# A decoder trunk on one core: the feed-forward norms by one matmul of ones and a power on 512 columns

## The chip, the cores and the metric

The kernel runs on 1 core of one Trainium2 chip. Its time is the device time of one execution in microseconds. TensorE (PE) does the matmuls, with its weight loads shown apart (PEld); VectorE (DVE), ScalarE (ACT) and GpSimd (POOL) do the rest of the arithmetic; SyncE (SP) and GpSimd issue most of the transfers. The median of three runs before is 1825.48 us (1823.81 to 1827.0).

## The reference

Two layers of a decoder trunk, 512 positions of 1024 numbers in float32, and a last norm. Each layer is a half-step feed-forward, a mixer and another half-step feed-forward, each behind an RMS norm:

```python
def _rmsnorm(x, g):
    y = xf * lax.rsqrt(jnp.mean(xf * xf, axis=-1, keepdims=True) + EPS)
    return (y * g.astype(jnp.float32)).astype(x.dtype)

def _swiglu(x, w_gate, w_up, w_down):
    return (jax.nn.silu(x @ w_gate) * (x @ w_up)) @ w_down

def _layer(x, ...):
    x = x + MACARON * _swiglu(_rmsnorm(x, ffn1_norm), ffn1_w_gate, ffn1_w_up, ffn1_w_down)
    h = _rmsnorm(x, mix_norm)
    p = h @ w_in
    ...                                     # three mixers on parts of p
    x = x + jnp.concatenate([y_a, y_b, y_c], axis=-1) @ w_out
    x = x + MACARON * _swiglu(_rmsnorm(x, ffn2_norm), ffn2_w_gate, ffn2_w_up, ffn2_w_down)
    return x
```

The feed-forwards are 1024 to 2816 and back. So there are six norms in the layers (four of feed-forwards, two of mixers) and the final one.

## The kernel before, in words

x lies on the chip transposed: features on the 128 partitions, the 512 positions along the columns, eight tiles of 128 features in four pairs. Every float32 operand of a large matmul is split into a high part (a cast on ScalarE) and a low part (a subtraction on VectorE, L90), and a product is three matmuls: high by high, high by low, low by high (L150 to L152, L257 to L259).

A feed-forward (`ffn`, and `last_ffn` in the last layer) works through the gate's and the up projection's columns in 22 "quads" q: 11 blocks of columns, gate (j = 0) and up (j = 1) in turn. A quad is seven products of half size (n = 1 to 7, Strassen's scheme with Winograd's sums), twelve matmuls of 128x256 each. `begin(q)` takes the quad's weights from a raw buffer, makes sums of them and splits them (`forms`), and fetches those of the next quad (`fetch`): four transfers a quad, three issued by SyncE and one, which adds to what is already there, by GpSimd (L112). There are two raw buffers.

The norm is put off behind the projections. x times the gain goes into the matmuls, and the result is multiplied by the reciprocal root of the mean square afterwards. That is `done(q)`: of a gate quad the whole tile is multiplied by the rows `rr` (L338), goes through Silu on ScalarE (L339), and is multiplied by `rr` again (L340); of an up quad the tile is multiplied by the gate (L343), and split into what the down projection takes.

`squares(m)` sums the squares of x over the eight tiles into `acc`, 128x512; the sum over the partitions is still to be done. The norm does it in two steps. `norm_columns` makes 128 positions at a time a column: four matmuls of acc by a column of ones give 128x4 in PSUM, VectorE divides by 1024 and adds epsilon (`ms`), and GpSimd raises it to the power -1/2 (`rc`, L230). `norm_rows` makes rows of the columns: four diagonal matrices (`dg`, L240) and four matmuls of ones by them (`psr`, L241) give every partition the same row of 512 numbers, which ScalarE copies (`rr`, L243). The mixers use both `rc` and `rr`.

In three feed-forwards the two steps are taken out of the list `norms` behind the first two products that follow the opening ones of quads 0 and 1. In the very first (`from_start`), the first two quads are computed by plain products in `start`, with the squares behind them; there the list has places to wait, and its last entry calls `norm_rows` and then `done(0)` and `done(1)`.

The order of instructions on each engine is not the order of the code: a scheduler sets it when the program is built. Each engine then works its own queue in order and waits at an instruction until what that needs is there.

Of the kernel before, what the change touches and what calls it, by code (L numbers as in the profile page):

```python
# [9 lines left out]
F32 = mybir.dt.float32  # L10
F32R = mybir.dt.float32r
AF = mybir.ActivationFunctionType
ALU = mybir.AluOpType
AX = mybir.AxisListType

P = 128
D = 1024
T = 512
# [8 lines left out]
EPS = 1e-6  # L27
# [21 lines left out]
def trunk(ctx, tc, xt, w_gu1, w_dn1, w_in, w_out, w_gu2, w_dn2, w_last, par, con, wst, bst, gain, out):  # L49
    nc = tc.nc  # L50
# [3 lines left out]
    spool = ctx.enter_context(tc.tile_pool(name="spool", bufs=2))  # L54
# [3 lines left out]
    def bank(name):  # L58
        return pp.tile([P, T], F32, tag="ps", name=name)
# [6 lines left out]
    def uniq(s):  # L66
        uid[0] += 1
        return f"{s}{uid[0]}"
# [8 lines left out]
    ones = cpool.tile([P, P], F32, name="ones")  # L77
    nc.vector.memset(ones, 1.0)
    mhalf = cpool.tile([P, 16], F32, name="mhalf")
# [77 lines left out]
    state = {}  # L157
# [12 lines left out]
    def scratch(i, name):  # L170

        if stage["tags"] is None:
            return big(uniq(name))
        if i == 2:
            return stage["pool"].tile([P, 4 * T], F32, tag="hp", name=uniq(name), bufs=4)
        return stage["pool"].tile([P, 2 * T], F32, tag=stage["tags"][i], name=uniq(name), bufs=2)
# [56 lines left out]
    def norm_rows():  # L233

        rc = state["rc"]
        pr = bank(uniq("psr"))
        dg = scratch(2, "dg")
        for n in range(NCH):
            d = dg[:, n * P : (n + 1) * P]
            nc.vector.tensor_scalar(d, ident, rc[:, n : n + 1], None, ALU.mult)  # L240
            nc.tensor.matmul(pr[:, n * P : (n + 1) * P], lhsT=ones, rhs=d, start=True, stop=True)  # L241
        rr = spool.tile([P, T], F32, tag="rr", name=uniq("rr"), bufs=1)
        nc.scalar.copy(rr, pr)  # L243
        state["rr"] = rr

    MOVING = {1: A11, 2: A12, 3: Z4, 4: A22, 5: S1, 6: S2, 7: S3}
# [26 lines left out]
    def gate_up(w_gu, first, others, tail, from_start=False):  # L275

        quads = [(p, j) for p in range(FP) for j in range(2)]
        steps = [(7 * q + t, 0, q, n) for q in range(len(quads)) for n, t in WHEN.items()]
        steps += [(t, 1, None, work) for t, work in others]
        steps.sort(key=lambda e: e[:2])
        live, gates, raws = {}, {}, {}

        def ahead(q):
            if q < len(quads) and q not in raws:  # L290
                raws[q] = fetch(w_gu[quads[q][0], quads[q][1]])

        def begin(q):
            p, j = quads[q]
            ahead(q)
            c = stage["pool"].tile([P, 2 * T], F32, tag="gu"[j], name=uniq("gu"[j]), bufs=2)
            live[q] = {"w": forms(raws[q]), "c": c}
            ahead(q + 1)

        def quarter(q, i):  # L300
            return live[q]["c"][:, i * H : (i + 1) * H]

        def psum(q, name):
            if name not in live[q]:
                live[q][name] = bank(uniq(name))[:, :H]
            return live[q][name]

        def matmuls(q, n, pairs=range(KP)):
            name = {1: "pa", 2: "pb", 3: "pc", 4: "pa", 5: "pc", 6: "pa", 7: "pa"}[n]
            fresh_bank = name not in live[q]  # L310
            product(psum(q, name), n, live[q]["w"], fresh_bank, pairs)

        def after(q, n):
            c11, c21, c12, c22 = [quarter(q, i) for i in range(4)]
            b = live[q]
            if n == 1:
                nc.scalar.copy(c11, b["pa"])  # L317
            elif n == 2:
                nc.vector.tensor_tensor(c11, b["pb"], c11, ALU.add)
            elif n == 6:  # L320
                nc.scalar.copy(c12, b["pa"])
            elif n == 5:
                nc.scalar.copy(c22, b["pc"])
            elif n == 7:
                nc.vector.tensor_tensor(c22, c22, b["pa"], ALU.subtract)
            elif n == 3:
                nc.vector.tensor_tensor(c12, b["pc"], c12, ALU.subtract)
            else:
                nc.scalar.copy(c21, b["pa"])
                done(q)  # L330

        def done(q):
            p, j = quads[q]
            c = live.pop(q)["c"]
            if j == 0:
                c3 = c.rearrange("p (f t) -> p f t", f=2)
                rr = state["rr"].unsqueeze(1).broadcast_to([P, 2, T])
                nc.vector.tensor_tensor(c3, c3, rr, ALU.mult)  # L338
                nc.scalar.activation(c, c, AF.Silu)  # L339
                nc.vector.tensor_tensor(c3, c3, rr, ALU.mult)  # L340
                gates[p] = c
            else:
                nc.vector.tensor_tensor(c, c, gates.pop(p), ALU.mult)  # L343
                h = stage["pool"].tile([P, 4 * T], F32R, tag="hp", name=uniq("h"), bufs=4)
                parts(h[:, : 2 * T], h[:, 2 * T :], c)
                for i in range(2):
                    first.append((h[:, i * T : (i + 1) * T], h[:, (2 + i) * T : (3 + i) * T]))

        if from_start:
            norms = start(w_gu, live, done)  # L350
            skip = lambda q, n: q < 2
        else:
            begin(0)
            begin(1)
            for m in range(KP):
                for q in (0, 1):
                    for n in (1, 2):
                        ps = psum(q, ("pa", "pb")[n - 1])
                        hi, lo = live[q]["w"][n]
                        bh, bl = form(m, MOVING[n])  # L360
                        c = slice(m * P, (m + 1) * P)
                        mm3(ps, hi[:, c], lo[:, c], bh, bl, m == 0, m == KP - 1, skip_group_check=True)
            for q in (0, 1):
                for n in (1, 2):
                    after(q, n)
            norms = [norm_columns, norm_rows]
            skip = lambda q, n: q < 2 and n < 3
        for _, kind, q, n in steps:
            if kind:
                n()  # L370
                continue
            if skip(q, n):
                continue
            if q not in live:
                begin(q)
            matmuls(q, n)
            if norms:
                norms.pop(0)()
            after(q, n)
        tail()  # L380

    def start(w_gu, live, done):

        for k in range(12):
            warm = warm_ps[:, (k % 4) * P : (k % 4 + 1) * P]
            nc.tensor.matmul(warm, lhsT=ones, rhs=ones, start=True, stop=True)
        pool = stage["pool"]  # L390
        extra = pool.tile([P, 4 * T], F32R, tag="hp", name="a21", bufs=4)
        a21 = [(extra[:, m * H : (m + 1) * H], extra[:, (4 + m) * H : (5 + m) * H]) for m in range(KP)]
        weights = {}
        for m in range(KP):
            nc.sync.dma_start(xp[m], xt[:, 2 * m : 2 * m + 2, :])
            norm_pair(m, G1, True)
            gained(m, 0, G1, a21[m][0], a21[m][1], slice(H, T))
            if m == 0:
                weights[0] = load_plain(w_gu[0, 0])
        weights[1] = load_plain(w_gu[0, 1])  # L400
        for m in range(KP):
            norm_sums(m, G1)
        for j in range(2):
            b11, b21, b22, b12 = weights[j]
            ps = [bank(uniq("pg")) for _ in range(2)]
            for m in range(KP):
                c = slice(m * P, (m + 1) * P)
                kw = {"skip_group_check": True}
                for i, w in ((0, b21), (1, b22)):
                    hi, lo = xf[m][:, H : 3 * H], xf[m][:, 8 * H : 10 * H]  # L410
                    mm3(ps[i], w[0][:, c], w[1][:, c], hi, lo, m == 0, False, **kw)
                for i, w in ((0, b11), (1, b12)):
                    for t, a in ((slice(0, H), form(m, A11)), (slice(H, T), a21[m])):
                        mm3(ps[i][:, t], w[0][:, c], w[1][:, c], a[0], a[1], False, m == KP - 1, **kw)
            c = pool.tile([P, 2 * T], F32, tag="gu"[j], name=uniq("gu"[j]), bufs=2)
            for i in range(2):
                nc.scalar.copy(c[:, i * T : (i + 1) * T], ps[i])
            live[j] = {"c": c}
        for m in range(KP):
            squares(m)  # L420

        def rows():
            norm_rows()
            done(0)
            done(1)

        wait = lambda: None
        return [wait] * 5 + [norm_columns] + [wait] * 2 + [rows]

    def schedule(l, w_dn, hs):  # L430

# [433 lines left out]
```

## Time and profile before

| | |
|---|---|
| median of three runs | 1825.48 us |
| the profiled execution | 1829.11 us |
| its span, first to last instruction | 1827.3 us |
| TensorE busy | 1808.7 us |
| VectorE busy | 1328.3 us |
| ScalarE busy | 832.2 us |
| GpSimd busy | 121.0 us |
| granted clock of TensorE, mean | 0.994 |

Times of the trace count from the span's first instruction. A row of a timeline gives start, duration, engine, line, operation, what is written and read, and in brackets how long the engine had been idle before and what it waited for. The four feed-forward norms stand at about 47, 575, 925 and 1478 us.

### The profile page before, as it was taken

To read this page: it belongs to the slowest core of one execution; us is meant where nothing else is said; L and a number is where in the kernel's file an instruction comes from. 1 tells how busy PE (TensorE), PEld (TensorE's weight loads), DVE (VectorE), ACT (ScalarE), POOL (GpSimd) and SP (SyncE) were. 2 spreads that over 40 slices of the span, in tenths; PEclk is the share of its full clock that TensorE was granted. 3 is DMA by queue.
4 is the path that set the end of the run, shared out by engine and by line. 5 is a ranking of instruction groups with operands and counts; after the bars stand their busy time and mean duration, and the time that the engine had idled before them with its cause. 6 is when DMAs were issued, how large, how long until landed. Compare 5 with 4: busy or idle time off the path is not lost.

```text
span 1827.3 us, 28699 instructions
## 1 busy us (share of the span) xinstructions
PE 1808.7 (99%) x11704; PEld 1655.4 (91%) x11704; DVE 1328.3 (73%) x1818; ACT 832.2 (46%) x1222; POOL 121.0 (7%) x120
## 2 busy tenths in 40 slices
PE   9999999999999999999999999999999999999998
PEld 8999999888889999999899999998888899999997
DVE  7877777675667777777878777766757678777765
ACT  6544444413345544444655444444133555444444
POOL 0100000000100000000000000000000000000000
PEclk9999999999999999999999999999999999999999
DMA  7655555522223765555446655564222157655532
GB/s 214 183 162 150 148 148 153 180 81 82 73 89 81 185 167 156 156 156 155 128 106 178 162 155 156 156 175 128 92 81 81 58 128 190 168 156 156 154 89 81
DMA packets 120339, 251.20 MB, mean 137 GB/s; under 512 B 9744, under 2 KB 11792, under 8 KB 119696
## 3 DMA queue, kind: packets, MB, share of 16 engines
q1 hardware_dynamic: 96672, 204.25, 34.6%
q0 software_dynamic: 23392, 45.09, 14.9%
q8 instruction: 91, 1.49, 0.3%
q14 instruction: 40, 0.33, 0.1%
q10 hardware_dynamic: 144, 0.04, 0.0%
HBM read 247.24 MB, written 2.10 MB: 136 GB/s over the span
## 4 chain that ended last, share of the span: by engine, by line
PE 93%; DVE 3%; DMA 2%; ACT 1%; issue 1%; SPq 0%; POOL 0%; POOLq 0%; ACTq 0%
PE pa L257 8%; PE pa L259 8%; PE pa L258 8%; PE pdn L150 8%; PE pdn L151 8%; PE pdn L152 8%; PE pc L259 4%; PE pc L257 4%; PE pc L258 4%; PE pb L257 2%; PE pb L259 2%; PE pb L258 2%; PE pqk L150 2%; PE pqk L152 2%; PE pout L150 2%; PE pout L152 2%
## 5 line engine op out<-in xcount | busy, mean ns | idle before, releaser
L150 PE MATMUL pdn<-h,wdn 128*128 128x512 f32 x632 | 248.2, 393 | 0.0
L151 PE MATMUL pdn<-h,wdn 128*128 128x512 f32 x632 | 248.0, 392 | 0.0
L152 PE MATMUL pdn<-h,wdn 128*128 128x512 f32 x632 | 246.6, 390 | 0.3 <-DVE wdn L90 0.3
L89 ACT CAST wd<-rawq 128x1024 fp32r<-128x1024 f32 (+1 forms) x172 | 135.0, 832 | 176.6 <-PE pc L259 171.3
L257 PE MATMUL pa<-xf,wa 128*128 128x256 f32 x688 | 196.5, 286 | 3.7 <-ACT u L317 2.9
L89 ACT CAST wdn<-rawd 128x512 fp32r<-128x512 f32 (+1 forms) x152 | 97.0, 638 | 218.0 <-PE pdn L152 189.0
L259 PE MATMUL pa<-xf,wa 128*128 128x256 f32 x688 | 195.8, 285 | 0.0
L258 PE MATMUL pa<-xf,wa 128*128 128x256 f32 x688 | 195.7, 284 | 0.0
L90 DVE TENSOR_TENSOR wd<-rawq,wd 128x1024 fp32r<-128x1024 f32 (+1 forms) x172 | 157.4, 955 | 49.3 <-ACT wd L89 49.1
L112 POOL DMA_DIRECT2D rawq<-in_w_gu x86 | 94.3, 1096 | 1271.3 <-DMA rawq<-in_w_gu 580.1
L89 ACT CAST w<-raw 128x1024 fp32r<-128x1024 f32 x77 | 80.9, 1051 | 196.3 <-PE pqk L152 60.6
L152 PEld LDWEIGHTS pdn<-h,wdn 128*128 128x128 f32 x632 | 119.0, 188 | 26.9 <-DVE wdn L90 1.1
L90 DVE TENSOR_TENSOR w<-raw,w 128x1024 fp32r<-128x1024 f32 x77 | 94.1, 1223 | 64.6 <-ACT w L89 63.9
L150 PEld LDWEIGHTS pdn<-h,wdn 128*128 128x128 f32 x632 | 119.6, 189 | 21.2
L151 PEld LDWEIGHTS pdn<-h,wdn 128*128 128x128 f32 x632 | 119.6, 189 | 19.6
L257 PEld LDWEIGHTS pa<-xf,wa 128*128 128x128 f32 x688 | 133.2, 194 | 4.5 <-ACT u L317 3.3
L258 PEld LDWEIGHTS pa<-xf,wa 128*128 128x128 f32 x688 | 133.3, 194 | 0.0
L259 PEld LDWEIGHTS pa<-xf,wa 128*128 128x128 f32 x688 | 133.1, 194 | 0.0
L90 DVE TENSOR_TENSOR wdn<-rawd,wdn 128x512 fp32r<-128x512 f32 (+1 forms) x152 | 107.0, 705 | 23.9 <-ACT wdn L89 23.9
L273 DVE SCALAR_TENSOR_TENSOR x<-pdn,x 128x512 f32<-128x512 f32 x152 | 104.1, 685 | 3.7 <-PE pdn L152 3.6
L90 DVE TENSOR_TENSOR wb<-rawq,wb 128x1024 fp32r<-128x1024 f32 x86 | 104.9, 1220 | 2.4 <-ACT wb L89 2.4
L90 DVE TENSOR_TENSOR wa<-rawq,wa 128x1024 fp32r<-128x1024 f32 x86 | 104.9, 1220 | 1.8 <-ACT wa L89 1.8
(289 smaller groups left out, 5080.9 us busy)
## 6 DMA issues: line engine op xcount, KB each, us to landing
rawq<-in_w_gu SPq DMA_DIRECT2D x172, 512.0 KB, 5.4
rawq<-in_w_gu POOLq DMA_DIRECT2D x86, 512.0 KB, 5.8
rawd<-in_w_dn SPq DMA_DIRECT2D x140, 256.0 KB, 5.0
raw<-in_w_in SPq DMA_DIRECT2D x52, 512.0 KB, 3.5
rawq<-in_w_gu SPq DMA_DIRECT2D x86, 256.0 KB, 5.9
raw<-in_w_out SPq DMA_DIRECT2D x16, 512.0 KB, 3.5
rawd<-in_w_dn SPq DMA_DIRECT2D x12, 384.0 KB, 3.3
raw<-in_w_last SPq DMA_DIRECT2D x6, 512.0 KB, 4.4
```

Source lines behind the costliest of these rows:

```text
L89: nc.scalar.copy(hi, src)
L90: nc.vector.tensor_tensor(lo, src, hi.bitcast(F32), ALU.subtract)
L112: nc.gpsimd.dma_start(two[:, :, 1, :], src.rearrange("p (n s c) -> p n s c", n=2, s=2)[:, :, 0, :], accum_op=ALU.add)
L150: nc.tensor.matmul(ps, lhsT=ah, rhs=bh, start=first, stop=False, **kw)
L151: nc.tensor.matmul(ps, lhsT=ah, rhs=bl, start=False, stop=False, **kw)
L152: nc.tensor.matmul(ps, lhsT=al, rhs=bh, start=False, stop=last, **kw)
L257: nc.tensor.matmul(ps, lhsT=hi[:, c], rhs=bh, start=one, stop=False, skip_group_check=True)
L258: nc.tensor.matmul(ps, lhsT=hi[:, c], rhs=bl, start=False, stop=False, skip_group_check=True)
L259: nc.tensor.matmul(ps, lhsT=lo[:, c], rhs=bh, start=False, stop=m == pairs[-1], skip_group_check=True)
L273: nc.vector.scalar_tensor_tensor(x[d], p, 0.5, x[d], ALU.mult, ALU.add)
```

## The change

The four feed-forward norms are computed by a new function, `norm_rows_alone`; the mixers keep `norm_columns` and `norm_rows`. One matmul with a 128x128 matrix of ones as the stationary operand sums `acc` over the partitions, and gives every partition the same row of 512 sums. VectorE divides by 1024 and adds epsilon, out of PSUM into `rr`; GpSimd raises `rr` in place to the power -1/2, 128x512 numbers. The tile of the diagonals is not needed there.

```diff
+    def norm_rows_alone():
+
+        ps = bank(uniq("psr"))
+        nc.tensor.matmul(ps, lhsT=ones, rhs=state["acc"], start=True, stop=True)
+        rr = spool.tile([P, T], F32, tag="rr", name=uniq("rr"), bufs=1)
+        nc.vector.tensor_scalar(rr, ps, 1.0 / D, EPS, ALU.mult, ALU.add)
+        nc.gpsimd.tensor_tensor(rr, rr, mhalf[:, 0:1].broadcast_to([P, T]), ALU.pow)
         state["rr"] = rr
...
-            norms = [norm_columns, norm_rows]
+            norms = [norm_rows_alone]
             skip = lambda q, n: q < 2 and n < 3
...
         def rows():
-            norm_rows()
+            norm_rows_alone()
             done(0)
             done(1)

         wait = lambda: None
-        return [wait] * 5 + [norm_columns] + [wait] * 2 + [rows]
+        return [wait] * 6 + [rows]
```

The lines behind the new function move down by nine: L338 becomes L347, L340 L349, L319 L328, L325 L334, L327 L336. Two places of the new order matter to what follows.

VectorE's queue in the second feed-forward, before, from the scaling of the norm's columns to the first reader of `rr`. `g` and `u` are the result tiles of the first gate and up quad, `wb` holds two operands of the second quad's weights, `wd` three of the third quad's; "waits" names the engine or transfer whose signal an instruction waits for:

```order
L228 TENSOR_SCALAR ms_5206<-pss_5201 128x4 [waits PE_49]
L240 TENSOR_SCALAR dg_5225<-ident,rc_5208 128x128 [waits Pool_49]
L319 TENSOR_TENSOR g_5095<-pb_5137,g_5095 128x256 [waits Activation_49]
L319 TENSOR_TENSOR u_5114<-pb_5145,u_5114 128x256 [waits Activation_49]
L240 TENSOR_SCALAR dg_5225<-ident,rc_5208 128x128 x3
L325 TENSOR_TENSOR g_5095<-g_5095,pa_5133 128x256 [waits PE_49,Activation_49]
L90 TENSOR_TENSOR wb_5125<-rawq_5109,wb_5125 128x1024 [waits Activation_49]
L327 TENSOR_TENSOR g_5095<-pc_5211,g_5095 128x256 [waits PE_49]
L90 TENSOR_TENSOR wd_5320<-rawq_5128,wd_5320 128x1024 [waits DMAHW3_49,Activation_49]
L90 TENSOR_TENSOR wd_5320<-rawq_5128,wd_5320 128x512 [waits DMAHW4_49,Activation_49]
L127 TENSOR_TENSOR rawq_5128<-rawq_5128 128x512 [waits DMASW6_49,DVE_49]
L130 TENSOR_TENSOR rawq_5128<-rawq_5128 128x512 [waits DVE_49]
```

The same stretch now, up to the first reader of `rr`:

```order
L251 TENSOR_SCALAR rr_5187<-psr_5185 128x512 [waits PE_49]
L328 TENSOR_TENSOR g_5079<-pb_5121,g_5079 128x256 [waits Activation_49]
L328 TENSOR_TENSOR u_5098<-pb_5129,u_5098 128x256 [waits Activation_49]
L334 TENSOR_TENSOR g_5079<-g_5079,pa_5117 128x256 [waits PE_49,Activation_49]
L90 TENSOR_TENSOR wb_5109<-rawq_5093,wb_5109 128x1024 [waits Activation_49]
L336 TENSOR_TENSOR g_5079<-pc_5191,g_5079 128x256 [waits PE_49]
L90 TENSOR_TENSOR wd_5288<-rawq_5112,wd_5288 128x1024 [waits DMAHW3_49,Activation_49]
L90 TENSOR_TENSOR wd_5288<-rawq_5112,wd_5288 128x512 [waits DMAHW4_49,Activation_49]
L127 TENSOR_TENSOR rawq_5112<-rawq_5112 128x512 [waits DMASW6_49,DVE_49]
L130 TENSOR_TENSOR rawq_5112<-rawq_5112 128x512 [waits DVE_49]
L347 TENSOR_TENSOR g_5079<-g_5079,rr_5187 128x1024 [waits Activation_49,Pool_49]
L334 TENSOR_TENSOR u_5098<-u_5098,pa_5125 128x256 [waits PE_49]
```

The diagonals are gone, and with them the wait for GpSimd at VectorE's second instruction; the wait for GpSimd now stands at L347, behind the same low parts and sums as before. The third and fourth feed-forwards have the same order here.

GpSimd's queue in the same place, before:

```order
L112 DMA rawq_5128<-in_w_gu 128x2x512 [waits DMAHW2_49,DMAHW6_49,DMASW4_49,DVE_49]
L230 TENSOR_TENSOR rc_5208<-ms_5206,mhalf 128x4 [waits DVE_49]
L112 DMA rawq_5333<-in_w_gu 128x2x512 [waits DMAHW3_49,DMAHW5_49,DMASW5_49,DVE_49]
L112 DMA rawq_5450<-in_w_gu 128x2x512 [waits DMAHW0_49,DMAHW3_49,DMASW6_49,DVE_49]
L112 DMA rawq_5566<-in_w_gu 128x2x512 [waits DMAHW3_49,DMAHW6_49,DMASW7_49,DVE_49]
```

And now:

```order
L112 DMA rawq_5112<-in_w_gu 128x2x512 [waits DMAHW2_49,DMAHW6_49,DMASW4_49,DVE_49]
L252 TENSOR_TENSOR rr_5187<-rr_5187,mhalf 128x512 [waits DVE_49]
L112 DMA rawq_5301<-in_w_gu 128x2x512 [waits DMAHW3_49,DMAHW5_49,DMASW5_49,DVE_49]
L112 DMA rawq_5418<-in_w_gu 128x2x512 [waits DMAHW0_49,DMAHW3_49,DMASW6_49,DVE_49]
L112 DMA rawq_5534<-in_w_gu 128x2x512 [waits DMAHW3_49,DMAHW6_49,DMASW7_49,DVE_49]
```

The power keeps its place between the third quad's fetch and the fourth's; only its size changes.

## Rows read from the trace of the kernel before

**Rows 1.** The page, busy time by engine: us (share of the span) xinstructions

```profile
PE 1808.7 (99%) x11704; PEld 1655.4 (91%) x11704; DVE 1328.3 (73%) x1818; ACT 832.2 (46%) x1222; POOL 121.0 (7%) x120
```

**Rows 2.** Powers by line: ns min/median/max, first and last start, shapes

```profile
L532 POOL TENSOR_TENSOR rf<-r,mhalf x4: 539/548/574, 1810.0 to 1822.3; 128x1 f32<-128x1 f32 x4
L769 POOL TENSOR_TENSOR rs<-var,mhalf x10: 1006/1008/2899, 455.4 to 1392.2; 128x4 f32<-128x4 f32 x8, 128x16 f32<-128x16 f32 x2
```

**Rows 3.** VectorE's timeline behind powers of 4, 16 and 1 columns

```profile
370.56 0.87 DVE L240 TENSOR_SCALAR dg<-ident,rc 128x128 f32<-128x128 f32 x4 [1.16 <-POOL rc L230]
...
458.29 1.23 DVE L770 TENSOR_TENSOR side<-side,rs 128x1024 f32<-128x1024 f32 x1 [3.01 <-POOL rs L769]
...
1814.73 0.49 DVE L534 TENSOR_SCALAR o<-o,rf 128x512 f32<-128x512 f32 x1 [0.67 <-POOL rf L532]
```

**Rows 4.** Timeline, VectorE and GpSimd: the two powers that took longer

```profile
48.55 1.23 DVE L90 TENSOR_TENSOR wd<-rawq,wd 128x1024 fp32r<-128x1024 f32 x1
48.73 1.96 POOL L230 TENSOR_TENSOR rc<-ms,mhalf 128x4 f32<-128x4 f32 x1 [8.39 <-DVE ms L228]
...
479.14 0.69 DVE L685 TENSOR_TENSOR sg<-yn,sg 128x512 f32<-128x512 f32 x1
479.31 1.39 POOL L769 TENSOR_TENSOR rs<-var,mhalf 128x4 f32<-128x4 f32 x1 [0.95 <-DVE mean L761]
```

**Rows 5.** Timeline, TensorE in the second feed-forward

```profile
574.95 1.05 PE L226 MATMUL pss<-ones,acc 128*128 128x1 f32 x8 [0.39 <-DVE acc L219]
...
578.82 1.05 PE L241 MATMUL psr<-dg,ones 128*128 128x128 f32 x8
...
584.26 0.28 PE L259 MATMUL pc<-xf,wb 128*128 128x256 f32 x1
...
592.90 0.28 PE L259 MATMUL pa<-xf,wa 128*128 128x256 f32 x1
```

**Rows 6.** Timeline, VectorE and GpSimd in the second feed-forward

```profile
576.04 0.16 DVE L228 TENSOR_SCALAR ms<-pss 128x4 f32<-128x4 f32 x1
576.30 1.03 POOL L230 TENSOR_TENSOR rc<-ms,mhalf 128x4 f32<-128x4 f32 x1 [3.06 <-DVE ms L228]
...
582.42 1.23 DVE L90 TENSOR_TENSOR wb<-rawq,wb 128x1024 fp32r<-128x1024 f32 x1 [0.59 <-ACT wb L89]
583.56 0.42 DVE L327 TENSOR_TENSOR g<-pc,g 128x256 f32<-128x256 f32 x1
...
587.50 1.22 DVE L338 TENSOR_TENSOR g<-g,rr 128x1024 f32<-128x1024 f32 x1 [0.34 <-ACT g L329]
...
588.98 1.22 DVE L90 TENSOR_TENSOR wa<-rawq,wa 128x1024 fp32r<-128x1024 f32 x1
```

**Rows 7.** Timeline, GpSimd and TensorE in the third and fourth feed-forwards

```profile
926.16 1.04 POOL L230 TENSOR_TENSOR rc<-ms,mhalf 128x4 f32<-128x4 f32 x1 [26.89 <-DVE ms L228]
...
935.62 0.28 PE L259 MATMUL pc<-xf,wb 128*128 128x256 f32 x1
...
1479.48 1.03 POOL L230 TENSOR_TENSOR rc<-ms,mhalf 128x4 f32<-128x4 f32 x1 [2.99 <-DVE ms L228]
...
1487.44 0.28 PE L259 MATMUL pc<-xf,wb 128*128 128x256 f32 x1
```

**Rows 8.** Timeline, TensorE in the first feed-forward

```profile
66.17 0.28 PE L257 MATMUL pa<-xf,wa 128*128 128x256 f32 x1
```

**Rows 9.** Windows: stretch, length, busy of PE, PEld, DVE, ACT, POOL, granted clock, transfers

```profile
6.00:8.00 2.00, 0.00 (x0) 0.00 (x0) 1.84 (x5) 1.80 (x4) 0.00 (x0) 1.00 0.99 408
8.80:15.20 6.40, 6.21 (x20) 5.20 (x21) 6.40 (x12) 6.40 (x14) 0.00 (x0) 0.50 0.96 352
49.20:52.80 3.60, 3.60 (x20) 3.60 (x19) 2.62 (x8) 0.00 (x0) 2.11 (x2) 0.53 0.82 262
```

**Rows 10.** The page: GpSimd's fetches (busy, mean ns); their size, median us to landing

```profile
L112 POOL DMA_DIRECT2D rawq<-in_w_gu x86 | 94.3, 1096 | 1271.3 <-DMA rawq<-in_w_gu 580.1
...
rawq<-in_w_gu POOLq DMA_DIRECT2D x86, 512.0 KB, 5.8
```

More of the change, by code (lines that the diff above doesn't have):

```diff
@@ L244, in norm_rows @@
         state["rr"] = rr
+    def norm_rows_alone():
[4 more added lines that the diff above has]
+        nc.gpsimd.tensor_tensor(rr, rr, mhalf[:, 0:1].broadcast_to([P, T]), ALU.pow)
+        state["rr"] = rr
     MOVING = {1: A11, 2: A12, 3: Z4, 4: A22, 5: S1, 6: S2, 7: S3}
```

## The prediction, made before the changed kernel ran

> **What bounds the kernel now.** I read the page's engine totals first: TensorE is busy for 1808.7 of the 1827.3 us span, VectorE for 73%, GpSimd for 7% [rows 1]. Whatever makes TensorE wait is therefore paid in full, and nothing later gives it back. Next I asked the trace for GpSimd's instructions by shape, since the change gives that engine 128 times as many columns [rows 2], and then for the instructions that waited for them [rows 3]. Last I read the timelines of TensorE, VectorE and GpSimd around the norms that change, for two things: how long after the norm TensorE runs on work that doesn't need it, and which VectorE instruction meets it first [rows 5 to 8].
>
> **What is removed and added.** Only the four feed-forward norms change; the two of the mixers keep their columns and diagonal. Each loses two groups of eight TensorE passes, busy for 1.05 us each [rows 5], a 0.16 us scaling and four diagonal products on VectorE, a 4-column power, and a copy on ScalarE. It gains one float32 matmul of 512 columns, a scaling of 512 columns and a power of 512 columns. The matmul is work of the kind and amount of the second removed group (four times 128 columns), so TensorE saves about the first group, 0.9 us; as TensorE then stands still, this saving is swallowed. The scaling is costed by VectorE's 0.49 us for 128x512 [last of rows 3] in place of 0.16 us, so +0.34 us on the path.
>
> **The power, the term that decides.** GpSimd needed 548 ns for 1 column, 1008 for 4 and 2899 for 16 (the medians, and the longest) [rows 2]. From 1 to 4 that is 153 ns a column, from 4 to 16 it is 158, from 1 to 16 it is (2899 - 548)/15 = 156.7. So 512 columns take 2.90 + 496 x 0.1567 = 80.6 us; the two other slopes give 78.8 and 81.1. These are not just a profiler's rough ends: VectorE's waits behind them grow alike, 0.67, 1.16 and 3.01 us [rows 3], or 156 ns a column from first to last. From below, no row forbids that a long operand runs no longer than the 16 columns did, 2.9 us. I take 80.6, since three points lie on one line.
>
> The Trainium skill ("GPSIMD Engine Reference", 3.1 Elementwise) gives some 2.6 cycles an element at 1.2 GHz for a two-input operation; an estimate from that page is 1.1 us for 512 columns, and by it the change would cost nothing (third rival). The rows of this power, 156 ns a column, are some 70 times dearer, and I go by the rows.
>
> **What stands behind it.** In the second feed-forward the new power can begin at 576.30 + 0.34 = 576.64 and ends at 657.24. VectorE's first reader of the norm's rows is the scaling of the first gate (L338 before, L347 now), which before started at 587.50 [rows 6]. Behind it on VectorE stand the subtraction for the other quad, the low parts of the next quad's weights and all that follows; on ScalarE the Silu, with the copies and casts behind it; on GpSimd the next weight fetch; on SyncE the fetch after that, when a buffer comes free. TensorE uses the first low part behind the reader at 592.90 [rows 5].
>
> But VectorE may stop sooner. The trace shows that a power and a VectorE instruction with two operands in SBUF don't run side by side: the power at 48.73 found such a low part (48.55, 1.23 us) running and took 1.96 us, that is 1.01 us after its end; the one at 479.31 found one of 0.69 us and took 1.39 [rows 4]. No row shows the other order, VectorE waiting for a running power, since a power of 1 us has no such instruction behind it. I take it to be the same both ways. Then in the last three feed-forwards VectorE stands not at L347 but at the low part of the second quad's weights, which started at 582.42 [rows 6] and which TensorE reads at 584.26 [rows 5]. The Trainium skill ("SBUF — State Buffer", Who interferes with whom) says just that: GpSimd and a VectorE instruction with two SBUF inputs share a port, and the first to come holds it for its whole instruction. The rows above agree for one direction; no run here shows the other.
>
> **The sum.** Second feed-forward: the power ends at 657.24, the low part takes 1.2 us, TensorE goes on at 658.44 where before it was at 584.26: +74.2 us. Third: 926.16 + 0.34 + 80.6 + 1.2 = 1008.3 against 935.62: +72.7. Fourth: 1479.48 + 82.14 = 1561.62 against 1487.44: +74.2 [rows 7].
>
> First feed-forward: its two first quads are finished from the start, so the order is another. Before, its power was begun at 48.73 [rows 4]; the wider scaling and a low part that now stands ahead of it make that about 49.3. The power ends at 129.9. Then VectorE does seven instructions of 1024 columns (1.2 us each), three of 512 (0.7) and one of 256 (0.4), 10.9 us [rows 4, 6], before the next quad's low part is there, at 140.8. Twenty matmuls later (0.12 us each: 72 of them lie between 584.26 and 592.90) TensorE is where it was at 66.17 [rows 8], and four matmuls further: 143.2 - 66.65 = +76.6.
>
> Clock: after TensorE had stood still from 6 to 8 us it was granted 0.50 from 8.80 to 15.20, the lower level of 1.2 GHz; a stretch right behind the first norm lasted 3.6 us at 0.53 [rows 9]. At half rate that loses 1.7 to 3.2 us a restart. I take 2.4, four times, 9.6 us.
>
> Hidden behind the restart: VectorE then needs 7.7 us to the next quad's low part (1.2 + 0.4 + 1.9 + 1.4 + 1.2 + 0.4 + 1.2), and TensorE reaches it 1.2 + 72 x 0.12 = 9.8 us after the power. The fetch behind the power takes 1.1 us on GpSimd and lands 5.8 us after that [rows 10], so 6.9 us after the power, and VectorE gets to its data some 12.8 us after (five more instructions, 5.1 us). Neither adds anything; a microsecond beyond these covers would be paid.
>
> Total: 76.6 + 74.2 + 72.7 + 74.2 + 9.6 = 307.3 us on a profiled execution of 1829.1 us, so 2136. That execution lay 3.6 us above the median of the runs, 1825.5; against the median it is **2133 us**.
>
> **Rivals.**
> *VectorE goes on beside the power (28%).* Then only L347 and what is behind it waits. For: no row shows the port held against VectorE. Against: the two powers that did wait. Second feed-forward: 657.24 plus the 1.5 us from that reader's start to the low part's start (587.50 to 588.98 before) plus 1.2 us = 659.9, against 592.90 [rows 5, 6]: +67.0. The other two lose as much less as this one, 7.2 us; the first about as before. Sum 307 - 22 = 285, time 2110 us.
>
> *The stall costs more than once (6%).* The weight fetch on GpSimd's queue stands behind the power, and were its data to come last after the restart, TensorE would stop again. It decides from 5.9 us (12.8 - 6.9) of delay on; at 6 us beyond that, four times, 2133 + 24 = 2157 us. Against: the queue is empty then and the median landing is 5.8 us.
>
> *The power of many columns streams (6%), the other side.* With 2.9 to 4 us it ends by about 581, 6 us ahead of L338's 587.50; nothing waits, TensorE is rid of 0.9 us in each feed-forward, and of about 1.7 us in the stretch at 0.53 if the column matmuls had a part in it. 1825.5 - 3.6 = 1822 us, or 1820. The point from which it turns is a power of about 6 us: where the port is held the low part at 582.42 comes late from there, otherwise from about 11. Against it stand three points on one line.
>
> *Something between (4%)*: a cost per column that falls with length, say 40 us a power, 1825.5 + 4 x 34 = 1960 us.
>
> **How the numbers follow.** Forecast 56%, the rest as given. Port held and not held lie close together, 2133 and 2110; with the slopes' ends (4 x 1.8 us down, 4 x 0.6 up) and the clock's (4 x 0.8) they span about 2098 to 2145. I let the range go from 2098 to 2152; what it leaves out are the streaming and the falling power and most of the repeated stall. About 0.2%, 4 us, is what a measurement of this kernel tells from no change. The streaming power gives half faster, half the same, 3% each; all else is slower, 94%.
>
> **What the new profile would show.** Four powers on GpSimd of 79 to 82 us, each behind a matmul of the sum; TensorE idle for some 70 us behind each, released through VectorE; VectorE waiting for GpSimd at its first two-input instruction in three of them (or at L347 in all, if the port is free); a granted clock of 0.5 for a few us after each restart; GpSimd busy 320 us more than now. A power of a few microseconds would make the forecast wrong from the root; powers of 80 us with TensorE hardly idle would mean that I misread what stands behind VectorE's wait.

## The result and the profile after

The changed kernel takes 2112.39 us (median; 2111.43 to 2113.99), the kernel before on the same chip 1826.24 us: a ratio of 1.1573, 95% interval 1.1550 to 1.1596. The profiled execution took 2111.58 us, its span is 2109.7 us, the mean granted clock 0.928.

The page first: busy time by engine, and the shares of the chain that ended last.

```profile
PE 1807.7 (86%) x11648; PEld 1652.3 (78%) x11648; DVE 1326.6 (63%) x1802; ACT 829.9 (39%) x1218; POOL 443.6 (21%) x120
...
PE 80%; POOL 16%; DVE 2%; issue 1%; ACT 1%; DMA 0%; POOLq 0%; SPq 0%; ACTq 0%
```

Against [rows 1], TensorE has as much work as before and is idle for 302 us of the span instead of 19. GpSimd has 323 us more, and holds 16% of the chain. The next rows are the page's groups: the new power, the first reader of its rows, and the Silu.

```profile
L252 POOL TENSOR_TENSOR rr<-rr,mhalf 128x512 f32<-128x512 f32 x4 | 327.8, 81960 | 43.5 <-DVE rr L251 43.5
...
L347 DVE TENSOR_TENSOR g<-g,rr 128x1024 f32<-128x1024 f32 x44 | 53.9, 1225 | 366.1 <-POOL rr L252 298.4 <-ACT g L338 67.7
...
L348 ACT ACTIVATE g<-g 128x1024 f32<-128x1024 f32 x44 | 46.4, 1056 | 292.7 <-DVE g L347 292.7
```

One power takes 81.96 us where one of 16 columns took 2.9 [rows 2], and VectorE waits 298.4 us for the four; the Silu on ScalarE waits 292.7 us for VectorE's L347 behind it. The waits of TensorE (total, times, longest) say how that reaches it:

```profile
PE pa L266 <- ACT g L326: 209.4, 4, 69.7
PE pc L266 <- ACT wb L89: 78.2, 1, 78.2
```

That is 78.2 us in the first feed-forward and about 69.6 us in each of the others. The engines' timelines in the second, where [rows 5, 6] show it before:

```profile
651.74 1.12 PE L249 MATMUL psr<-acc,ones 128*128 128x512 f32 x2 [0.40 <-DVE acc L219]
...
652.90 0.69 DVE L251 TENSOR_SCALAR rr<-psr 128x512 f32<-128x512 f32 x1
...
653.68 81.96 POOL L252 TENSOR_TENSOR rr<-rr,mhalf 128x512 f32<-128x512 f32 x1 [3.37 <-DVE rr L251]
...
735.67 1.23 DVE L347 TENSOR_TENSOR g<-g,rr 128x1024 f32<-128x1024 f32 x1 [72.64 <-POOL rr L252]
...
737.15 1.22 DVE L90 TENSOR_TENSOR wa<-rawq,wa 128x1024 fp32r<-128x1024 f32 x1
...
736.93 1.06 ACT L348 ACTIVATE g<-g 128x1024 f32<-128x1024 f32 x1 [70.18 <-DVE g L347]
737.90 0.35 ACT L326 COPY g<-pa 128x256 f32<-128x256 f32 x1
...
738.30 0.58 PE L266 MATMUL pa<-xf,wa 128*128 128x256 f32 x1 [69.62 <-ACT g L326]
```

The power ends at 735.64 and VectorE starts L347 at once. Nothing that TensorE waits for needs the norm. It waits for ScalarE's copy L326, which frees a PSUM bank, and that copy stands in ScalarE's queue behind the Silu, which needs L347. Read upward, the chain is power, L347, Silu, copy, matmul. TensorE stopped at 738.30 - 69.62 = 668.68, 15.0 us after the power began, and goes on 2.7 us behind its end.

In the first feed-forward TensorE waits for a cast of weights (`wb`, L89), which stands in the same queue behind the Silu:

```profile
131.39 1.06 ACT L348 ACTIVATE g<-g 128x1024 f32<-128x1024 f32 x1 [79.71 <-DVE g L347]
...
133.56 1.04 ACT L89 CAST wb<-rawq 128x1024 fp32r<-128x1024 f32 x1
...
134.65 0.58 PE L266 MATMUL pc<-xf,wb 128*128 128x256 f32 x1 [78.20 <-ACT wb L89]
```

Windows of the first stall, of the time from each restart until the clock is back, and of a stretch behind that (length, busy of PE, PEld, DVE, ACT, POOL, granted clock, DMA share, GB/s):

```profile
60.00:130.00 70.00, 0.00 (x0) 0.00 (x0) 0.00 (x0) 0.00 (x0) 70.00 (x1) 0.50 0.00 0
...
134.65:142.04 7.39, 5.92 (x24) 5.34 (x25) 7.39 (x10) 4.22 (x6) 0.00 (x0) 0.50 0.03 6
738.30:742.78 4.48, 4.48 (x21) 4.48 (x22) 4.48 (x7) 1.79 (x3) 0.00 (x0) 0.50 0.93 192
1155.41:1159.21 3.80, 3.80 (x18) 3.80 (x19) 3.80 (x6) 1.79 (x3) 0.00 (x0) 0.50 1.01 210
1776.40:1780.43 4.03, 4.03 (x19) 4.03 (x20) 4.03 (x6) 1.80 (x3) 0.00 (x0) 0.50 0.98 199
...
743.00:745.00 2.00, 2.00 (x19) 2.00 (x18) 1.42 (x3) 0.51 (x2) 0.29 (x1) 1.00 0.95 340
```

From 60 to 130 only GpSimd works. Behind each stall TensorE runs for 3.8 to 5.9 us at 0.50, the level of 1.2 GHz. Half of that time is lost, 9.1 us in the four.

### The profile page after: what moved, and what is told of

It reads as the page before. It is cut to its first block, busy times and chain, and to the rows that moved or that the text cites. A ratio compares the mean times of both kernels' runs of the same rounds, so it can differ in the third digit from the quotient of the medians.

```text
span 2109.7 us, 28571 instructions
## 1 busy us (share of the span) xinstructions
PE 1807.7 (86%) x11648; PEld 1652.3 (78%) x11648; DVE 1326.6 (63%) x1802; ACT 829.9 (39%) x1218; POOL 443.6 (21%) x120
## 4 chain that ended last, share of the span: by engine, by line
PE 80%; POOL 16%; DVE 2%; issue 1%; ACT 1%; DMA 0%; POOLq 0%; SPq 0%; ACTq 0%
POOL rr L252 16%; PE pa L266 7%; PE pa L267 7%; PE pa L268 7%; PE pdn L150 7%; PE pdn L151 7%; PE pdn L152 7%; PE pc L268 4%; PE pc L267 4%; PE pc L266 4%; PE pb L267 2%; PE pb L266 2%; PE pb L268 2%; PE pqk L150 1%; PE pqk L151 1%; PE pout L151 1%
## 5 line engine op out<-in xcount | busy, mean ns | idle before, releaser
L252 POOL TENSOR_TENSOR rr<-rr,mhalf 128x512 f32<-128x512 f32 x4 | 327.8, 81960 | 43.5 <-DVE rr L251 43.5
L347 DVE TENSOR_TENSOR g<-g,rr 128x1024 f32<-128x1024 f32 x44 | 53.9, 1225 | 366.1 <-POOL rr L252 298.4
L89 ACT CAST wd<-rawq 128x1024 fp32r<-128x1024 f32 (+1 forms) x172 | 135.3, 832 | 174.7 <-PE pc L268 170.6
L89 ACT CAST wdn<-rawd 128x512 fp32r<-128x512 f32 (+1 forms) x152 | 96.9, 638 | 212.5 <-PE pdn L152 191.6
L266 PE MATMUL pc<-xf,wb 128*128 128x256 f32 x344 | 99.4, 289 | 78.2 <-ACT wb L89 78.2
L348 ACT ACTIVATE g<-g 128x1024 f32<-128x1024 f32 x44 | 46.4, 1056 | 292.7 <-DVE g L347 292.7
L89 ACT CAST w<-raw 128x1024 fp32r<-128x1024 f32 x77 | 80.9, 1051 | 196.1 <-PE pqk L152 60.6
```

Source lines behind the costliest of these rows:

```text
L89: nc.scalar.copy(hi, src)
L252: nc.gpsimd.tensor_tensor(rr, rr, mhalf[:, 0:1].broadcast_to([P, T]), ALU.pow)
L266: nc.tensor.matmul(ps, lhsT=hi[:, c], rhs=bh, start=one, stop=False, skip_group_check=True)
```

## The experiments

My theory was by then: all of the loss is the power's length, 0.159 us a column, and it is paid beyond a fixed cover, since L347 waits in VectorE's queue and the Silu in ScalarE's. The rivals: that the new order or the wide matmul has a part in it, that the price goes by numbers and not by columns, and my own forecast, that VectorE is also shut out by the port. The variants without the power, with the square root and with the logarithm have the median of twelve executions; the others ran once.

**Without the power.**

```diff
-        nc.vector.tensor_scalar(rr, ps, 1.0 / D, EPS, ALU.mult, ALU.add)
-        nc.gpsimd.tensor_tensor(rr, rr, mhalf[:, 0:1].broadcast_to([P, T]), ALU.pow)
+        nc.vector.tensor_scalar(rr, ps, 1e-3 / D, EPS, ALU.mult, ALU.add)
```

> The changed kernel without the four powers; the scaling divides by 1024000 instead of 1024, so the rows of the norm are not the norm here: the reciprocal root is what is left out. Theory A (all of the loss is the wait for the power, the rest of the change is a small gain): TensorE has no idle stretch of more than about 3 us at the norms, and the time is that of the kernel before less four times the 0.9 to 1.2 us of TensorE's work that the one matmul saves, 1821 to 1823 us. Theory B (part of the loss is the new order of the queues or the matmul of 512 columns itself): the time stays above that of the kernel before, 1830 us or more.

Measured: 1820.01 us beside 1826.60 for the kernel before, ratio 0.9969 (0.9956 to 0.9982). Theory A holds, and the rest of the change is a gain of 6.6 us, more than the 3.6 to 4.8 that I gave it: the time lies just under the range. The profile shows TensorE busy for

```profile
PE 1800.2 (99%) x11648; PEld 1644.9 (91%) x11648; DVE 1326.2 (73%) x1802; ACT 829.5 (46%) x1218; POOL 115.7 (6%) x116
```

of a span of 1815.9. That closes the sum for the power: the changed kernel's span is 293.8 us longer, 286.3 of it more idle time (302.0 against 15.7) and 7.5 more busy time. The four restarts lose 9.1 us by the clock; against that, this run had the lower clock for longer in its opening (0.51 from 7.67 to 14.50, the changed kernel 0.52 from 8.80 to 12.30).

Part of the 6.6 us may be the clock too. The kernel before was granted half the clock in three more stretches of some 3.5 us: at 49.2 [rows 9], at 626 and at 926. This kernel had none of them, and the changed one has none but behind its stalls. I thought the column matmuls the likely cause; the rows don't bear that out. The first two lines are of the kernel before, the third of this one, the last of the variant with the square root below:

```profile
575.00:579.00 4.00, 4.00 (x34) 4.00 (x35) 2.74 (x8) 0.57 (x2) 1.03 (x1) 1.00 0.52 93
626.00:629.50 3.50, 3.50 (x14) 2.92 (x13) 3.50 (x7) 1.35 (x3) 0.00 (x0) 0.52 0.62 159
...
17.00:1810.00 1793.00, 1787.58 (x11591) 1633.63 (x11589) 1313.21 (x1777) 814.78 (x1196) 114.50 (x109) 1.00 0.51 137
...
59.50:66.00 6.50, 4.65 (x22) 4.44 (x23) 6.50 (x9) 2.52 (x5) 0.00 (x0) 0.61 0.25 63
```

The second norm's column matmuls ran at 1.00. The stretch at 626 has no norm near it, and follows a wait of TensorE of 1.99 us. The variant with the root has no such matmuls there and was granted 0.61 for 6.5 us. What brings these stretches stays open.

**Powers of 64, 128, 256 and 384 columns.**

```diff
-        nc.vector.tensor_scalar(rr, ps, 1.0 / D, EPS, ALU.mult, ALU.add)
-        nc.gpsimd.tensor_tensor(rr, rr, mhalf[:, 0:1].broadcast_to([P, T]), ALU.pow)
+        nc.vector.tensor_scalar(rr, ps, 1e-3 / D, EPS, ALU.mult, ALU.add)
+        n = state.setdefault("widths", [64, 128, 256, 384]).pop(0)
+        nc.gpsimd.tensor_tensor(rr[:, :n], rr[:, :n], mhalf[:, 0:1].broadcast_to([P, n]), ALU.pow)
```

> The power on the first 64, 128, 256 and 384 columns of the row in the first to fourth feed-forward; the other columns are left without it. Theory A (GpSimd takes the same time for each further column, 0.159 us, and only what is longer than TensorE's remaining work is paid): powers of 10.5, 20.7, 41.1 and 61.4 us. In the changed kernel TensorE stopped 15.0 us after the power began in the second feed-forward and went on 2.6 us behind its end, so a power of 12.4 us would be hidden there; in the first it stopped 8.3 us after the start and went on 4.6 us behind the end, so 3.7 us are hidden. Stalls of 6.8, 8.3, 28.7 and 49.0 us follow, 93 in sum, with 1 to 2.4 us a restart for the clock and 4.6 us saved by the matmul: 1918 to 1924 us. Theory B (a long operand has a price that grows faster or slower than its columns, or a stall costs by its being there and not by its length): the four lengths don't lie on one line of about 0.159 us a column, or the stalls are not the lengths less the same cover.

Measured: 1917.74 us, just under the range of 1918 to 1924. GpSimd's and TensorE's timelines, one pair for each feed-forward:

```profile
48.43 10.56 POOL L253 TENSOR_TENSOR rr<-rr,mhalf 128x64 f32<-128x64 f32 x1 [9.15 <-DVE rr L251]
...
582.81 20.75 POOL L253 TENSOR_TENSOR rr<-rr,mhalf 128x128 f32<-128x128 f32 x1 [3.63 <-DVE rr L251]
...
938.50 41.15 POOL L253 TENSOR_TENSOR rr<-rr,mhalf 128x256 f32<-128x256 f32 x1 [27.45 <-DVE rr L251]
...
1518.47 61.55 POOL L253 TENSOR_TENSOR rr<-rr,mhalf 128x384 f32<-128x384 f32 x1 [3.43 <-DVE rr L251]
...
63.65 0.58 PE L267 MATMUL pc<-xf,wb 128*128 128x256 f32 x1 [6.89 <-ACT wb L89]
...
606.23 0.58 PE L267 MATMUL pa<-xf,wa 128*128 128x256 f32 x1 [8.42 <-ACT g L327]
...
982.31 0.58 PE L267 MATMUL pa<-xf,wa 128*128 128x256 f32 x1 [28.89 <-ACT g L327]
...
1582.69 0.58 PE L267 MATMUL pa<-xf,wa 128*128 128x256 f32 x1 [49.23 <-ACT g L327]
```

From 64 to 384 columns the power grows by 50.99 us, 0.1593 a column, and from each width to the next by the same. In the last three feed-forwards length less stall is 12.3, 12.3 and 12.3 us: that is the cover, and beyond it every microsecond is paid. In the first the cover is 3.7 (10.56 less 6.89).

**The sum in one partition.** The column of ones gives one row; scaling and power work on 1x512; a matmul by a row of ones spreads it.

```diff
...
-        nc.tensor.matmul(ps, lhsT=ones, rhs=state["acc"], start=True, stop=True)
+        nc.tensor.matmul(ps[0:1, :], lhsT=ones[:, 0:1], rhs=state["acc"], start=True, stop=True)
...
-        nc.gpsimd.tensor_tensor(rr, rr, mhalf[:, 0:1].broadcast_to([P, T]), ALU.pow)
+        nc.gpsimd.tensor_tensor(rr[0:1, :], rr[0:1, :], mhalf[0:1, 0:1].broadcast_to([1, T]), ALU.pow)
+        pr = bank(uniq("psr"))
+        nc.tensor.matmul(pr, lhsT=ones[0:1, :], rhs=rr[0:1, :], start=True, stop=True)
+        nc.scalar.copy(rr, pr)
```

> The sum goes into one partition only (a column of ones as the stationary operand), scaling and power work on 1x512 there, and a matmul by a row of ones gives the row to all partitions. Theory A (the power's price goes by the columns, whatever the partitions): four powers of 82 us as in the changed kernel, and TensorE, whose matmul of the row stands 12 to 18 matmuls behind the sum, waits some 80 us each time: 2150 to 2170 us. Theory B (the price goes by the numbers, which are worked one after another, and 128 partitions cost a multiple of one): the power takes from 1 to 10 us, and TensorE waits 0 to 10 us at the matmul of the row: 1825 to 1870 us.

Measured: 2163.32 us. The group of the power, busy time and mean:

```profile
L252 POOL TENSOR_TENSOR rr<-rr,mhalf 1x512 f32<-1x512 f32 x4 | 328.5, 82134 | 42.4 <-DVE rr L251 42.4
```

and TensorE's wait for it, now at the matmul that spreads the row:

```profile
PE psr L254 <- POOL rr L252: 325.2, 4, 81.6
```

One partition costs what 128 do, at 512 columns. The price is one of columns, so the same 512 powers cost 1.03 us as 128x4 [rows 6] and 82 as a row. The Trainium skill ("GPSIMD Engine Reference", 3.1 Elementwise) has 2.6 cycles an element for a two-input operation, and by that an estimate for 512 columns is 1.1 us; this power took 82.

**Two-operand additions beside the power.** Behind the power stand:

```diff
+        for i in range(8):
+            nc.vector.tensor_tensor(state["acc"], state["acc"], xp[0][:, :T], ALU.add)
```

> The changed kernel, with eight VectorE additions of two operands in SBUF (128x512, 0.69 us each when alone) put behind the start of each power; what they add to is not read again, so the calculation is the same. Theory A (a running power keeps such an instruction waiting only at the power's start): the first that overlaps the start is up to 0.8 us longer, all others take 0.69 us while the power goes on for 82 us; the first reader of the power's rows comes when it did, and the time is that of the changed kernel, 2110 to 2118 us. Theory B (my forecast: a power holds the port for its whole length): the first addition, or the first low part behind it, stands some 80 us, the low parts come late behind the power, and the time goes to 2130 us or more.

Measured: 2125.60 us, between what the two theories gave. The rows decide, not the time. VectorE and GpSimd in the first two feed-forwards:

```profile
47.91 0.68 DVE L254 TENSOR_TENSOR acc<-acc,x 128x512 f32<-128x512 f32 x1
48.09 82.34 POOL L252 TENSOR_TENSOR rr<-rr,mhalf 128x512 f32<-128x512 f32 x1 [9.06 <-DVE rr L251]
48.85 1.19 DVE L254 TENSOR_TENSOR acc<-acc,x 128x512 f32<-128x512 f32 x1
...
658.15 81.96 POOL L252 TENSOR_TENSOR rr<-rr,mhalf 128x512 f32<-128x512 f32 x1 [3.15 <-DVE rr L251]
658.64 1.10 DVE L254 TENSOR_TENSOR acc<-acc,x 128x512 f32<-128x512 f32 x1
...
659.77 0.69 DVE L254 TENSOR_TENSOR acc<-acc,x 128x512 f32<-128x512 f32 x1
...
662.89 0.69 DVE L254 TENSOR_TENSOR acc<-acc,x 128x512 f32<-128x512 f32 x1
663.50 1.22 DVE L90 TENSOR_TENSOR wb<-rawq,wb 128x1024 fp32r<-128x1024 f32 x1
...
666.17 1.82 DVE L90 TENSOR_TENSOR wd<-rawq,wd 128x1024 fp32r<-128x1024 f32 x2
```

The power at 48.09 found an addition running and took 0.4 us longer; the addition 0.76 us behind its start took 0.5 us longer. The one at 658.64, 0.49 us behind the start of the second power, lost 0.4; the next lost nothing. From about a microsecond behind the start, additions and low parts take their usual 0.69 and 1.22 us, while the power goes on for 80. Theory B falls. The last of them ended 9.8 us behind the power's start; how such an instruction fares later in the power no run here shows, since VectorE then has none until L347's turn.

That the time lies 13 us above the changed kernel's is VectorE's queue: in the first feed-forward six of the additions fall behind the power's end, among the instructions that TensorE waits for.

```profile
PE pa L268 <- DVE u L336: 221.6, 3, 84.9
PE pa L268 <- ACT g L328: 71.2, 1, 71.2
```

The longest wait is 84.9 us instead of 78.2. All of TensorE's waits at the norms come to 10 us more than in the changed kernel, and 3.5 us more of busy time go with them. My expectation hadn't counted that.

**The first feed-forward alone.**

```diff
-            norms = [norm_rows_alone]
+            norms = [norm_columns, norm_rows]
```

> Only the first feed-forward has the new norm; the other three keep the columns, the diagonals and the power of 4 columns. Theory A (each power is paid by itself, where it stands): the first stall of the changed kernel was 78.2 us, with 1.5 us of small waits and about 2 us of half clock behind it; less 1 to 2 us that the one matmul saves there: 1826 + 80 = 1904 to 1909 us, and no wait of more than 3 us in the other three. Theory B (a long stall lets the transfers run ahead and is partly given back later): 1895 us or less.

Measured: 1908.16 us beside 1828.25, with the wait of 78.2 us as in the changed kernel and no longer one than 2.6 elsewhere. The first stall costs alone what it costs there; nothing is given back.

**The root on ScalarE.**

```diff
+    eps = cpool.tile([P, 1], F32, name="eps")
+    nc.vector.memset(eps, EPS)
...
-        nc.vector.tensor_scalar(rr, ps, 1.0 / D, EPS, ALU.mult, ALU.add)
-        nc.gpsimd.tensor_tensor(rr, rr, mhalf[:, 0:1].broadcast_to([P, T]), ALU.pow)
+        nc.scalar.activation(rr, ps, AF.Sqrt, bias=eps[:, 0:1], scale=1.0 / D)
+        nc.vector.reciprocal(rr, rr)
```

> The whole calculation, with the one matmul kept: ScalarE takes the square root out of PSUM (scale 1/1024, epsilon as bias) and VectorE the reciprocal of 512 columns, instead of the scaling and GpSimd's power. Theory A (only the power's length makes the loss): ScalarE pays a table load of 1.28 us before the root and one of the same length for the next Silu, VectorE 0.7 us or some times that for the reciprocal, all inside the 12.4 us that lie hidden in the last three feed-forwards and 3.7 us in the first; TensorE saves about 1.2 us four times: 1820 to 1825 us. Theory B (the reciprocal or the table load stands in VectorE's or ScalarE's queue ahead of what TensorE waits for): every microsecond more than the cover is paid, four times; with a reciprocal of 5 us, 1830 to 1840 us.

Measured: 1824.90 us beside 1826.60, ratio 0.9984 (0.9971 to 0.9997). With the power gone the whole loss is gone, with the calculation complete. The reciprocal took 3.35 us:

```profile
L254 DVE RECIPROCAL rr<-rr 128x512 f32<-128x512 f32 x4 | 13.4, 3353 | 3.6 <-ACT rr L253 3.6
```

**Logarithm and exponential,** with the tile `eps` as in the last:

```diff
...
-        nc.vector.tensor_scalar(rr, ps, 1.0 / D, EPS, ALU.mult, ALU.add)
-        nc.gpsimd.tensor_tensor(rr, rr, mhalf[:, 0:1].broadcast_to([P, T]), ALU.pow)
+        nc.scalar.activation(rr, ps, AF.Ln, bias=eps[:, 0:1], scale=1.0 / D)
+        nc.scalar.activation(rr, rr, AF.Exp, scale=-0.5)
```

> The whole calculation with the one matmul, and the reciprocal root by ScalarE alone: the logarithm out of PSUM (scale 1/1024, epsilon as bias), then the exponential of -1/2 times it. The root with VectorE's reciprocal took 0.69 and 3.35 us and two table loads of 1.28 us, and its time lay 5 us above the variant without the power. Theory A (those 5 us are the reciprocal on VectorE's queue): without it, with a third table load, 1819 to 1823 us. Theory B (they are the table loads, which stand in ScalarE's queue ahead of the copies that free TensorE's banks): three loads instead of two make it 1826 to 1829 us.

Measured: 1823.83 us beside 1828.25, ratio 0.9979 (0.9966 to 0.9991): 0.2%, or 4.4 us, less than the kernel before, and some 288 less than the change. ScalarE in the first feed-forward:

```profile
47.86 1.28 ACT L253 ACT_TABLE_LOAD   x1
49.15 0.69 ACT L253 ACTIVATE rr<-psr,eps 128x512 f32<-128x512 f32 x1
49.86 1.28 ACT L254 ACT_TABLE_LOAD   x1
51.15 0.63 ACT L254 ACTIVATE rr<-rr 128x512 f32<-128x512 f32 x1
51.69 0.35 ACT L332 COPY u<-pa 128x256 f32<-128x256 f32 x1
52.06 1.28 ACT L350 ACT_TABLE_LOAD   x1
```

Root and loads are over by 53.34, and TensorE waits 0.52 us for the copy at 51.69. Its idle time in the whole span is 19.1 us (1821.2 less 1802.1 busy) beside 15.7 without the power, so most of the loads is hidden, but not all. The time lies between the two forecasts, above A's 1819 to 1823 and below B's 1826 to 1829. The intervals of this variant and the last overlap, so that the reciprocal is what the other loses stays unproved.

## Why the prediction was right and where it was wrong

The time lay inside the range and on the side forecast, but by the rival to which I gave 28%, not by the forecast's own mechanism. The range held both, since they lie only 23 us apart; that it was right is owed to the power's price and to the range's width, and as to the port it was luck.

- *The power.* Three short powers on one line gave 80.6 us; it took 81.96, and between 64 and 384 columns the slope is 0.159, not 0.157. The step was right, 1.4 us short each time.
- *The port, the step that failed.* "I take it to be the same both ways": I let VectorE's next low part stand for the power's whole length. It didn't. The rows on which I rested [rows 4] were of powers of 1 us, in which "the whole instruction" and "its first microsecond" are the same thing. (The first of them ended 0.91 us behind the low part's end, not 1.01.) The changed kernel has the other order in the first feed-forward, a low part of 0.69 us that began 0.15 behind the power, and in the second a low part 4.6 us into the power:

```profile
48.28 1.43 DVE L90 TENSOR_TENSOR wd<-rawq,wd 128x512 fp32r<-128x512 f32 x1
...
658.29 1.23 DVE L90 TENSOR_TENSOR wb<-rawq,wb 128x1024 fp32r<-128x1024 f32 x1 [0.59 <-ACT wb L89]
```

  The first lost 0.74 us, the second nothing. The Trainium skill ("SBUF — State Buffer", Who interferes with whom) says that the first to come keeps the shared port for its whole instruction; for this power the measurement differs, as far as it reaches, and decides. The step was worth 22 us, nearly all of the distance from 2133 to 2112.
- *The rival's own sum.* It gave 2110 us. It had the power 5.4 us too short in sum and the scaling at 0.49 instead of 0.69 us (0.8). The clock was right, 9.6 us where the restarts' windows show 9.1. Two things pulled the other way. The first power began at 48.13, not at about 49.3. And in the traced execution the kernel before lost some 3.7 us behind the second norm that the changed one doesn't lose, this wait and 1.7 us by the half clock from 626 (above):

```profile
625.05 0.39 PE L257 MATMUL pa<-xf,wa 128*128 128x256 f32 x1 [1.99 <-ACT u L317]
```

  So it is in part luck that the sum came within 3 us.
- *What stands behind VectorE's wait.* L347 first, then the Silu and the copies behind it, as said. That TensorE is let go by the low part was not: the copy L326 freed it, at 738.25. The low part was done at 738.37, so this moved nothing.
- *First feed-forward.* I had +76.6 us and 2.4 of clock for the matmul four behind the one at 66.17 [rows 8], at 66.65; it starts at 144.01 now, +77.4 with the clock in it.
- *What was to be hidden.* Fetch and next low part cost nothing: behind each restart no wait of more than 1.1 us follows.
- *The matmul.* I put its saving at 0.9 us, swallowed by the stall. It is 2.1 - 1.12 = 1.0; without the power the whole form gives 6.6 us, and what more than four times 1.0 brings is not settled.
- *Streaming, falling price, repeated stall.* None came. The point from which a power is paid, about 11 us by the rival's working, is 12.3 in the last three feed-forwards and 3.7 in the first.

## What to carry to other kernels

Before an elementwise operation is moved to another layout, ask by what its engine charges: GpSimd's power charges by columns, and the other partitions are free, so it belongs where the numbers fill the partitions. Extrapolate from two or three sizes in the trace, and read the cover (from the start of the slow work to where TensorE stops, less the way back) before choosing the size. Where a lock or a queue is argued from short instructions, look for a long one, since a short one can't tell "throughout" from "at the start".

## What the runs showed of the hardware

- A GpSimd power costs 0.159 us a column between 64 and 512 columns, and at 512 the same on 1 and on 128 partitions.
- A running power of 82 us delays a VectorE instruction of two SBUF operands by 0.4 to 0.74 us in its first microsecond, and not from 1.6 to 9.8 us behind its start. With one partition the low part 0.17 us behind the start took its usual 0.67, and the instruction 0.87 us behind it lost 0.73. An instruction of one SBUF and one PSUM operand (L328, 0.16 us behind the start) took its usual 0.41.
- A float32 matmul of 128x512 is two passes, 1.12 us in all, where eight passes of 128x1 or 128x128 took 1.05 [rows 5].
- Out of PSUM the scaling of 128x512 took 0.69 us, where one out of SBUF took 0.49 [rows 3]; VectorE's reciprocal of the same size took 3.35, ScalarE's logarithm out of PSUM 0.69.
